# A hybrid decoder block on one core: the recurrent branch's output projection as seven block products per two banks of tokens

## The chip, the cores and the metric

The kernel runs on one core of a Trainium2 chip. TensorE (PE) multiplies, VectorE (DVE), ScalarE (ACT) and GpSimd (POOL) do the elementwise work, and SyncE (SP) issues most DMAs. The metric is the device time of one execution in microseconds (us); lower is better.

## What is computed

One layer of a block with two parallel branches over 2048 tokens of width 1024, all in float32. Cut to what matters here:

```python
h = rms_norm(x, g_norm) * (1 + scale) + shift
x_rnn, z_rnn, q, k, v, z_attn, g_r, g_a = split(h @ w_in)
hr = rg_lru(causal_conv(x_rnn), ...)
y_rnn  = (hr * silu(z_rnn)) @ w_out_rnn        # 2048 x 1024 times 1024 x 1024
o = dilated_attention_mixture(rope(q), rope(k), v)
y_attn = (o * silu(z_attn)) @ w_out_attn
merged = sigmoid(g_r + b_r) * y_rnn + sigmoid(g_a + b_a) * y_attn
out = rms_norm(x + gate * (merged @ w_o), g_final)
```

The change concerns `y_rnn`, the product of the recurrent branch with `w_out_rnn`.

## The kernel before

**Precision.** Each float32 operand is split into a rounded high part and the rest, its low part. A product of two operands is three matmuls (`mm3`, line 154): high by high, high by low, low by high. A split is two operations: the high part by ACT (`hi_act`, 159) or by a DVE reduction over one element (1777), the low part by POOL (`lo_pool`, 165) or DVE (`lo_dve`, 168).

**Stages.** The tokens are two halves of two banks of 512. For each half the input projection runs as pairs of column blocks, each by the seven products of a Strassen-Winograd scheme (`strassen`, 355; products on operands B11, T2, T3, T1, B21, T4, B22). A product is four `mm3`. Small work, such as loads, splits, stores and the recurrence, is hung on product numbers (`after_prod`, `late`, lines 224 to 234; `later`, 1253) and issued when that product has been. At the end of the second half the last 42 products are the rotary pairs of q and k with four plain pairs between them (1363 to 1373). Beside them `residual_gate` (1257) computes the gate vector from eight loads of 512 KB, added by DVE.

**Attention with a fill.** Attention runs in slots, 96 units of scores plus lead-in and lead-out. Between its pieces each slot issues steps of a generator `fill` (`steps`, 1731), which does the output projections: a step is one `mm3` of 512 tokens (line 1840). The rate is `FILL` steps per slot, 2.85 in the first half's heads and 2.75 in the second's (lines 35 and 1888), with a few more at the start. `spend` issues them in three places of a slot: two after the scores, one after the transposes. Everything there is in an order written out by hand, so every engine, and SP's queue, works in program order.

**The fill's jobs.** Four jobs for the recurrent branch (one per bank, from `yaT`), then four for attention (from `oT`), of which the first lies in the slots and the last three follow as a tail of 192 steps, beside which the output projection's weights are built. A job is 64 steps: eight row blocks m of the result, each summed over eight k in one of two `pj` PSUM tiles. Weights come already split from `wD`, 512 KB for half a column of blocks. They are split and stored earlier, beside the second half's input projection (`output_weights`, 428). The operands y of a job are eight tiles of 256 KB; their loads and splits sit at fixed steps around the start of the job (`LOAD_Y`, `SPLIT_Y`, 1871), in nine buffer pairs `yh`, `yl`. `evict` (1792) multiplies a finished tile by its gate, loaded from `grT`, and `store` writes it to `mrT`.

**Winograd's terms.** In the change the same seven products are used for `y_rnn`. B11, B12, B21 and B22 are the blocks of the operand, upper or lower half of the rows by first or second bank of the half; T1 to T4 are their sums and differences.

## Time and profile before

| | |
|---|---|
| median of three runs | 2160.47 us (2158.46 to 2162.48) |
| the profiled execution, its own time | 2161.23 us |
| its span, first to last instruction | 2159.4 us |
| mean granted TensorE clock | 0.998 |
| busy, share of the span | PE 99%, DVE 68%, ACT 60%, POOL 52% |

By stage, from the windows and the timelines: the first half's projection to about 752 us, the second half's to about 1340, attention with the fill from 1340 to 1865, the tail of the fill, then the output projection to the end. PE's busy time counts overlapping matmuls once, so it says that something was under way, not that PE ran at its peak rate. A group's row gives line, engine, operation, output from inputs, shape, count, then busy time and mean time of one, then the idle time of the engine ahead of it and what ended that.

### The profile page before, as it was taken

The page shows a single profiled execution, that of the slowest core. Times are in us where ns is not written, and L with a number is a line of the kernel's source. Part 1 is how long each engine was busy: PE and PEld are TensorE (multiplying, and loading weights), DVE is VectorE, ACT ScalarE, POOL GpSimd, SP SyncE. Part 2 cuts the span into 40 slices and gives each one's busy share as a digit, 9 for nine tenths or more (in the row PEclk, how much of TensorE's full clock was granted, in tenths as well). Part 3 has the DMA queues.
Part 4 walks back from the last instruction along what each step waited for, and adds up shares of the span by engine and source line. Part 5 has one row for each costly group of instructions (what it writes and reads, how often), then busy time and mean ns, then how long its engine had stood idle before and what let it go on. Part 6 is the DMA issues. An engine that isn't in the chain of part 4 may idle for free.

```text
span 2159.4 us, 32571 instructions
## 1 busy us (share of the span) xinstructions
PE 2136.6 (99%) x10539; PEld 1788.3 (83%) x10539; DVE 1463.3 (68%) x2582; ACT 1296.2 (60%) x2592; POOL 1120.6 (52%) x868
## 2 busy tenths in 40 slices
PE   9999999999999999999999999999999999999998
PEld 6888778888888888888888887889898988878887
DVE  6759878768656715544436684587777687788777
ACT  5748668668644527457457532677788888443333
POOL 1467667777666423223223675466666664432555
PEclk9999999999999999999999999999999999999999
DMA  8467887887655368899997676888887777899543
GB/s 301 142 211 256 280 290 264 288 294 244 174 115 166 108 229 291 301 305 311 323 318 240 152 173 171 300 269 263 273 275 218 256 236 239 300 316 300 181 170 114
DMA packets 416575, 521.39 MB, mean 241 GB/s; under 512 B 107574, under 2 KB 282898, under 8 KB 415380
## 3 DMA queue, kind: packets, MB, share of 16 engines
q1 hardware_dynamic: 376388, 401.65, 59.7%
q10 hardware_dynamic: 34384, 99.78, 12.2%
q0 software_dynamic: 5632, 17.88, 2.6%
q8 instruction: 83, 1.36, 0.3%
q14 instruction: 88, 0.72, 0.1%
HBM read 332.02 MB, written 187.17 MB: 240 GB/s over the span
## 4 chain that ended last, share of the span: by engine, by line
PE 71%; DVE 4%; DMA 3%; issue 1%; POOL 1%; ACT 1%; SPq 0%; ACTq 0%; POOLq 0%; DVEq 0%
PE X L152 14%; PE V L152 13%; PE pj L152 12%; PE Z L152 7%; PE W L152 7%; PE Y L152 6%; PE sc L152 4%; PE o L152 4%; PE pg L152 1%; PE pT L1568 1%; PE pT L1581 1%; DMA fg<-gaT 1%; DMA kraw<-kqT 1%; DVE ptl L169 1%; DVE yl L169 1%
## 5 line engine op out<-in xcount | busy, mean ns | idle before, releaser
L166 POOL TENSOR_TENSOR S<-R,S 128x512 fp32r<-128x512 f32 x192 | 295.3, 1546 | 169.3 <-ACT S L160 82.9
L152 PE MATMUL V<-T,S 128*128 128x512 f32 x1344 | 324.3, 390 | 1.9 <-DVE ev L461 1.9
L152 PE MATMUL X<-T,S 128*128 128x512 f32 x1344 | 323.8, 390 | 1.6 <-ACT u L391 1.3
L152 PE MATMUL pj<-yh,S 128*128 128x512 f32 x896 | 321.6, 402 | 1.3 <-DVE fg L1795 0.8
L152 PEld LDWEIGHTS X<-T,S 128*128 128x128 f32 x1344 | 251.8, 188 | 56.5 <-ACT u L391 2.9
L152 PEld LDWEIGHTS V<-T,S 128*128 128x128 f32 x1344 | 251.9, 188 | 55.9 <-issue 1.9
L166 POOL TENSOR_TENSOR S<-s,S 128x512 fp32r<-128x512 f32 x116 | 173.3, 1494 | 150.1 <-ACT S L160 114.3
L152 PEld LDWEIGHTS pj<-yh,S 128*128 128x128 f32 x896 | 168.3, 188 | 32.3 <-DVE S L169 1.3
L1481 ACT ACTIVATE pp<-pp,st 128x256 f32<-128x256 f32 (+3 forms) x256 | 133.8, 524 | 78.0 <-DVE st L1480 77.4
L152 PE MATMUL pj<-yl,S 128*128 128x512 f32 x448 | 175.5, 392 | 1.0 <-POOL yl L166 1.0
L160 ACT ACTIVATE S<-s 128x512 fp32r<-128x512 f32 x124 | 77.3, 624 | 145.1 <-DVE s L291 92.1
L152 PE MATMUL W<-T,S 128*128 128x512 f32 x672 | 161.6, 389 | 0.0
L152 PE MATMUL Y<-T,S 128*128 128x512 f32 x672 | 161.6, 389 | 0.0
L152 PE MATMUL Z<-T,S 128*128 128x512 f32 x672 | 161.4, 389 | 0.0
L160 ACT ACTIVATE S<-R 128x512 fp32r<-128x512 f32 x200 | 121.5, 622 | 59.0 <-DMA R<-in_w_in_dram 14.8
L169 DVE TENSOR_TENSOR ptl<-pT,pth 128x384 fp32r<-128x384 f32 (+1 forms) x160 | 97.8, 628 | 80.5 <-ACT pth L160 78.4
L152 PEld LDWEIGHTS W<-T,S 128*128 128x128 f32 x672 | 126.0, 188 | 26.9 <-issue 0.9
L152 PEld LDWEIGHTS Z<-T,S 128*128 128x128 f32 x672 | 126.2, 188 | 26.2
L152 PEld LDWEIGHTS Y<-T,S 128*128 128x128 f32 x672 | 126.1, 188 | 26.1
L166 POOL TENSOR_TENSOR s<-R,s 128x512 fp32r<-128x512 f32 x32 | 43.2, 1350 | 188.8 <-ACT s L160 164.6
L980 DVE SCALAR_TENSOR_TENSOR xc<-xr,par,xc 128x512 f32<-128x512 f32 x96 | 102.0, 1062 | 52.1 <-ACT xc L974 49.9
L1548 ACT ACTIVATE pp<-pp,M 128x256 f32<-128x256 f32 (+3 forms) x256 | 118.0, 523 | 12.8 <-DVE M L1680 12.8
(419 smaller groups left out, 4906.0 us busy)
## 6 DMA issues: line engine op xcount, KB each, us to landing
sD<-S ACTq DMA_DIRECT2D x140, 512.0 KB, 3.7
S<-sD SPq DMA_DIRECT2D x140, 512.0 KB, 5.0
S<-wD SPq DMA_DIRECT2D x82, 512.0 KB, 5.5
R<-in_w_in_dram SPq DMA_DIRECT2D x144, 256.0 KB, 3.3
wD<-s ACTq DMA_DIRECT2D x64, 256.0 KB, 5.1
kraw<-kqT SPq DMA_DIRECT2D x32, 384.0 KB, 5.1
T<-in_w_mod_dram SPq DMA_DIRECT2D x16, 512.0 KB, 9.1
vN<-ev SPq DMA_DIRECT2D x32, 256.0 KB, 2.7
```

Of the source, the lines that this page charges most:

```text
L152: nc.tensor.matmul(o, lhsT=l, rhs=r, start=st, stop=sp, **kw)
L160: nc.scalar.activation(o, i, AF.Copy)
L166: nc.gpsimd.tensor_tensor(o, i, h.bitcast(F32), ALU.subtract)
L169: return nc.vector.tensor_tensor(o, i, h.bitcast(F32), ALU.subtract).ins
L980: nc.vector.scalar_tensor_tensor(xc, xr[:, i : i + CH], cw(i), xc, ALU.mult, ALU.add)
L1481: nc.scalar.activation(pdst, pdst, AF.Exp, bias=m_, scale=-1.0, accum_out=l_)
L1548: nc.scalar.activation(pp, pp, AF.Copy, scale=w)
L1568: nc.tensor.transpose(pt[:, c0 + j * P : c0 + (j + 1) * P], pp[i][:, k * P : (k + 1) * P], ident)
L1581: nc.tensor.transpose(pt[:, c * P : (c + 1) * P], pp[:, half * P : (half + 1) * P], ident)
```

## The change

The recurrent branch's four jobs become two rounds (one per half of the tokens) of seven block products. A block product is 4 row blocks p by 4 k, that is 16 steps. Its four PSUM tiles are not summed over products in PSUM: each is evicted on its own (`block_evict`), and running sums are kept in SBUF (`U`, `Q`). B11 is copied to U; T2 and T1 are added to U, T3 plus U goes to Q; B21, T1, T4 and B22 complete one of the four results, which is multiplied by its gate and stored.

- The weights are combined into seven blocks per pair of row blocks, split and stored in `wB` by `output_weights`: 28 blocks of 512 KB instead of 16 tiles, with 16 DVE combinations. The attention weights follow at a pitch of 3 products instead of 4.
- The operand sums T1 to T4 are made by `block_sums` beside the last 42 products of the input projection: eight groups, each with four loads, two DVE and two POOL subtracts and four stores of 256 KB to `tB`. The gate's adds are cut to halves of the width and spread over more products.
- An operand takes one of seven buffer pairs (14 tiles; four more hold U). Each block loads the next one's operands behind its steps 1, 4, 7 and 12, and splits at step 1 its own fourth operand, at 6, 9 and 12 the next one's first three. High parts are made by DVE, or by ACT for the even ones of the first round; low parts by POOL.
- `FILL` becomes 2.54 and 2.44.

The core of the diff:

```diff
-FILL = (2.85, 2.75)
+FILL = (2.54, 2.44)
...
+    BLOCKS = (("B11", 0), ("B21", 4), ("T2", 1), ("T3", 2), ("T1", 3), ("T4", 5), ("B22", 6))
+    N_WB = 2 * 7 * KH
...
     def output_weights():
+        n0, PITCH = n_prod[0], 3
...
+        for p in range(KH):
+            v, b = {}, 7 * PITCH * p + (4 * PITCH if p > 1 else 0)
+            load = block_loads([w_out_rnn[0][:, 2 * p * P : 2 * (p + 1) * P]])
+            for d, name, i, half in ((1, "a22", 1, 1), (4, "a21", 1, 0), (6, "a11", 0, 0), (8, "a12", 0, 1)):
+                on_n(b + d, lambda v=v, load=load, name=name, i=i, half=half: v.__setitem__(name, load(i, half)))
...
+            for x, (i, name, *sums) in enumerate((
+                (5, "a22"), (3, "a22", "a21", "a22", ALU.add), (0, "a11"), (1, "a22", "a22", "a11", ALU.subtract),
+                (2, "a21", "a11", "a21", ALU.subtract), (4, "a12"), (6, "a12", "a12", "a22", ALU.subtract))):
+                if sums:
+                    on_n(b + 5 + PITCH * x, lambda combine=combine, name=name, sums=sums: combine(name, *sums))
+                split_and_store(b + 5 + PITCH * x, lambda v=v, name=name: v[name], wB[i, p])
...
+    def block_sums(ep):
+        def load(g, half, j):
+            q, k = divmod(g, KH)
+            n = 2 * q + j
+            raws[g, half, j] = t = T(ep, [P, CH], F32, "bs", bufs=5)
+            nc.sync.dma_start(t[:], yaT[(half * KH + k) * P : (half * KH + k + 1) * P, n * CH : (n + 1) * CH])
+        def combine(g, dst, a, b, eng):
+            eng.tensor_tensor(raws[g, *dst][:], raws[g, *a][:], raws[g, *b][:], ALU.subtract)
+        def store(g, i, src):
+            q, k = divmod(g, KH)
+            nc.scalar.dma_start(tB[q, i, k], raws.pop((g, *src))[:])
+        b11, b12, b21, b22 = (0, 0), (0, 1), (1, 0), (1, 1)
+        dve, pool = nc.vector, nc.gpsimd
+        for g in range(2 * KH):
+            for d, fn, *args in ((-2, load, *b12), (-2, load, *b11), (-2, load, *b22), (-1, load, *b21),
+                                 (0, combine, b11, b12, b11, dve), (0, combine, b12, b22, b12, pool),
+                                 (1, combine, b22, b22, b11, dve), (1, store, 0, b11), (1, store, 2, b12),
+                                 (2, combine, b21, b21, b22, pool), (2, store, 1, b22), (3, store, 3, b21)):
+                later(3 + 5 * g + d, lambda fn=fn, g=g, args=args: fn(g, *args))
...
+        def operand(n, raw=None):
+            g, k = divmod(n, KH)
+            if g < 14:
+                q, (name, _) = g // 7, BLOCKS[g % 7]
+                h, l = OT[n] = fl_pair(n % 7)
...
+        def split(n, raw=None):
+            if n < 14 * KH:
+                h, l = OT[n]
+                src = l[:].bitcast(F32) if raw is None else raw[:]
+                if raw is not None or n % 2 == 0 and n < 7 * KH:
+                    hi_act(h[:], src)
+                else:
+                    nc.vector.tensor_reduce(h[:], src.unsqueeze(2), AX.X, ALU.max)
+                (lo_dve if raw is not None and n > 4 else lo_pool)(l[:], src, h[:])
+        OUT = {"B21": (0, 0), "T1": (1, 1), "T4": (1, 0), "B22": (0, 1)}
...
+        def block_evict(g, p, ps):
+            name = BLOCKS[g % 7][0]
+            tt = nc.vector.tensor_tensor
+            if name == "B11":
+                U[p] = T(fl, [P, CH], F32, f"F{14 + p}")
+                nc.vector.tensor_copy(U[p][:], ps[:])
+            elif name in ("T2", "T1"):
+                tt(U[p][:], ps[:], U[p][:], ALU.add)
+            elif name == "T3":
+                Q[p] = T(pR, [P, CH], F32, f"R{p}")
+                tt(Q[p][:], ps[:], U[p][:], ALU.add)
+            if name in OUT:
+                t = G[g, p]
+                tt(ps[:], ps[:], (Q if OUT[name][0] else U)[p][:], ALU.add)
+                tt(t[:], ps[:], t[:], ALU.mult)
...
+        for g in range(14):
+            for p in range(KH):
+                ps = T(pj, [P, CH], F32, "pj")
+                x = KH * g + p
+                for k in range(KH):
+                    j = KH * p + k
+                    if k == 1:
+                        (load_wb(x + 3) if x + 3 < N_WB else load_w(x + 3 - N_WB))
+                        if last:
+                            block_evict(*last)
...
+                    w, (yh, yl) = W[x], OT[KH * g + k]
+                    mm3(ps[:], w[:, 0, k, :], w[:, 1, k, :], yh[:], yl[:], first=k == 0, last=k == KH - 1)
+                    if k == KH - 1:
+                        W.pop(x)
+                    n = KH * (g + 1)
+                    for at_, k1 in ((1, 0), (4, 1), (7, 2), (12, 3)):
+                        if j == at_ and n + k1 > 6:
+                            operand(n + k1)
+                    for at_, n1 in ((1, n - 1), (6, n), (9, n + 1), (12, n + 2)):
+                        if j == at_ and n1 > 6:
+                            split(n1)
...
+                    yield
+                last = g, p, ps
```

193 lines of the change are left out of this document (125 added, 68 removed).

## The prediction

> **What bounds the kernel now.** I read the page first, its shares and its forty slices, then the chain that ended last, then the windows by stage.
>
> ```profile
> PE 2136.6 (99%) x10539; PEld 1788.3 (83%) x10539; DVE 1463.3 (68%) x2582; ACT 1296.2 (60%) x2592; POOL 1120.6 (52%) x868
> PEclk9999999999999999999999999999999999999999
> L152 PE MATMUL pj<-yh,S 128*128 128x512 f32 x896 | 321.6, 402 | 1.3 <-DVE fg L1795 0.8
> ```
>
> The last row is two thirds of the output projections (the high half of y meets both halves of the weights; the low half is the other third). Its 402 ns is a latency and not a price, since matmuls overlap. The price comes from the chain, where twelve of them follow each other without a gap:
>
> ```profile
> 788.07 2.72 PE W L152 x12
> ```
>
> 2.72/12 = 0.2267 us for each 512-column matmul, so one step (three matmuls, line 1840) costs 0.68 us. Whether steps can be saved at that price depends on whether TensorE is full in the stage they lie in.
>
> ```profile
> 780.00:1130.00 350.00, 350.00 (x1543) 289.44 (x1542) 164.74 (x224) 198.62 (x307) 99.21 (x76) 1.00 0.92 307
> 1226.00:1300.00 74.00, 74.00 (x328) 61.29 (x327) 54.77 (x66) 23.56 (x43) 49.76 (x33) 1.00 0.75 177
> 1300.00:1340.00 40.00, 40.00 (x172) 31.20 (x171) 20.68 (x27) 11.04 (x20) 23.24 (x16) 1.00 0.59 167
> 1340.00:1865.00 525.00, 519.34 (x3359) 464.51 (x3358) 380.21 (x1099) 399.72 (x1113) 311.39 (x270) 1.00 0.82 259
> 1422.00:1494.00 72.00, 72.00 (x491) 65.23 (x490) 50.92 (x176) 57.12 (x186) 44.99 (x47) 1.00 0.84 267
> 1404.00:1422.00 18.00, 17.16 (x114) 14.89 (x113) 17.38 (x48) 13.27 (x41) 11.61 (x11) 1.00 0.89 264
> 1512.00:1530.00 18.00, 17.33 (x115) 14.83 (x114) 16.24 (x49) 12.46 (x40) 9.36 (x9) 1.00 0.92 283
> 1620.00:1638.00 18.00, 15.55 (x99) 13.69 (x97) 14.00 (x41) 12.11 (x33) 13.18 (x13) 0.93 0.67 198
> ```
>
> Columns: length; busy time and instructions of PE, weight loads, DVE, ACT, POOL; clock; DMA share; GB/s. The first three stretches are the input projection of the second half. The fourth is attention with 320 output-projection steps filled in. In the quiet fifth, attention runs at 491/72 = 6.8 matmuls per us without idle time; so TensorE binds there, and a step removed is 0.68 us gained. The last three are the joints between jobs of 64 steps, where eight operands are split within some twenty steps: DVE reaches 17.38 of 18 us and TensorE gets 114, 115 and 99 matmuls where 123 would fit.
>
> **The matmuls.** Before, the recurrent branch takes 4 banks x 8 x 8 = 256 steps. After, 2 x 7 products x 16 = 224. 32 steps x 0.68 = 21.8 us less. The Trainium skill ("TensorE: Matmul & The Clock Gate", Back-to-back issue gap) gives about 131 ns for a 512-column matmul in a sustained stream; by it the saving would be 12.6 us (an estimate). The trace has 226.7 ns here, so its number stands.
>
> **The fill rate.** Slots now take 2.54 and 2.44 steps instead of 2.85 and 2.75. Summed over slots that gives the 288 steps needed, so nothing is left over or moves to the tail. The quiet slot shrinks from 72 us/(46 steps/2.85) = 4.46 to about 4.25 us by the shares (138 of its 491 matmuls write pj).
>
> ```profile
> 1422.00:1494.00 72.00, 38.71 (x138) 23.59 (x138) 4.11 (x6) 1.00 0.84 267
> L1795 DVE TENSOR_TENSOR fg<-pj,fg 128x512 f32<-128x512 f32 x40 | 27.3, 683 | 0.5 <-PE pj L152 0.5
> L1777 DVE TENSOR_REDUCE yh<-R 128x512 fp32r<-128x512 f32 x32 | 21.5, 677 | 0.0
> L166 POOL TENSOR_TENSOR yl<-R,yh 128x512 fp32r<-128x512 f32 x21 | 27.6, 1314 | 19.1 <-DMA vraw<-vN 5.6 <-DVE yh L1777 4.4 <-PE sc L152 3.2
> L169 DVE TENSOR_TENSOR yl<-R,yh 128x512 fp32r<-128x512 f32 x18 | 17.3, 967 | 0.6
> ```
>
> **Evictions.** Each output tile was one multiply of 683 ns, 32 in all. Now every product tile has its own: one operation for B11, T2 and T3, three for T1, two for B21, T4 and B22, that is 12 per pair of rows and 96 in all. 64 x 0.683 = 43.7 us more on DVE.
>
> **Splits.** 56 operands instead of 32. DVE reduces go from 24 to 39 (+10.2 us), DVE low parts from 15 to 2 (-12.6 us at 967 ns), POOL low parts from 17 to 54 (+48.6 us at 1314 ns), ACT high parts from 8 to 17 (ACT is busy 400 of 525). So DVE gains some 41 us and POOL 49 in a stage where they are busy 380 and 311 of 525: none reaches the stage's length on average. By block it is closer. A block of 16 steps lasts 6.3 slots, 26.8 us. DVE has (50.92 - 4.11)/16.1 = 2.9 us a slot of attention, 18.3 a block; a T1 block adds 12 x 0.683 + 4 x 0.677, to 29.2 us, so it is full; B21, T4 and B22 come to 26.5 and B11, T2, T3 to 23.7. I charge 1 us for the two T1 blocks, because DVE catches up while TensorE stands in the waits below; bounds 0 and 5 (the excess of 2.4 us, twice).
>
> **The new wait.** This decides. The fourth operand of each block lies in the buffer of the first operand of the block before, so its load is issued behind step 12, its split only behind step 1 (DVE reduce, then POOL), and step 3 multiplies it: one whole step lies between, where the old table leaves two. TensorE runs in order, so transposes, sums and scores queue behind a late low part. How long does such a split take from the end of the step that issued it?
>
> ```profile
> 1393.53 0.40 PE L152 MATMUL pj<-yh,S 128*128 128x512 f32 x1
> 1393.13 0.68 DVE L1777 TENSOR_REDUCE yh<-R 128x512 fp32r<-128x512 f32 x1
> 1396.72 1.31 POOL L166 TENSOR_TENSOR yl<-R,yh 128x512 fp32r<-128x512 f32 x1
> 1414.87 0.39 PE L152 MATMUL pj<-yh,S 128*128 128x512 f32 x1
> 1415.33 0.62 PE L152 MATMUL pj<-yh,S 128*128 128x512 f32 x2
> 1416.03 0.40 PE L152 MATMUL pj<-yh,S 128*128 128x512 f32 x1
> 1416.84 0.39 PE L152 MATMUL pj<-yl,S 128*128 128x512 f32 x1
> 1417.06 0.39 PE L152 MATMUL pj<-yh,S 128*128 128x512 f32 x1
> 1418.94 0.68 DVE L1777 TENSOR_REDUCE yh<-R 128x512 fp32r<-128x512 f32 x1
> 1419.38 0.40 PE L152 MATMUL pj<-yh,S 128*128 128x512 f32 x1
> 1419.76 1.29 POOL L166 TENSOR_TENSOR yl<-R,yh 128x512 fp32r<-128x512 f32 x1 [1.85 <-PE sc L152]
> 1419.85 0.62 PE L152 MATMUL pj<-yh,S 128*128 128x512 f32 x2
> 1421.10 0.50 PE L152 MATMUL pj<-yl,S 128*128 128x512 f32 x1 [0.62 <-POOL yl L166]
> 1731.53 0.39 PE L152 MATMUL pj<-yh,S 128*128 128x512 f32 x1
> 1733.77 0.68 DVE L1777 TENSOR_REDUCE yh<-R 128x512 fp32r<-128x512 f32 x1
> 1734.53 1.30 POOL L166 TENSOR_TENSOR yl<-R,yh 128x512 fp32r<-128x512 f32 x1 [2.58 <-DVE yh L1777]
> ```
>
> The timelines of TensorE, DVE and POOL hold 16 POOL splits behind a reduce, four of which stand alone; these are the first and the last of the four, and between them one from a joint. Step end to low part done: 1398.03 - 1393.76 = 4.3, 1421.05 - 1416.26 = 4.8, 1735.83 - 1731.76 = 4.1 us. The four alone, as the new ones mostly stand, average 3.6, all sixteen 4.6. The middle one shows the mechanism at work: it had two steps between, and TensorE still waited 0.62 us. What lead is there with one step? A slot issues its steps in three places: two in a row after the scores (A, B), one after the transposes (C), then sums and scores follow. From these rows: a split behind A is needed in C, 1416.84 - 1415.56 = 1.3 us later; behind B in the next A, 1419.61 - 1416.26 = 3.4; behind C in the next B, 1420.31 - 1417.29 = 3.0. The pacing code with the new rates puts the thirteen blocks' step 1 at A followed by B and C three times (2.9 us short each), behind B three times (0.8 twice, 0 in the longer slots of the second half), behind C before A and B twice (1.2 each), behind C with a skipped place or in the longer slots three times (0.3 each), and twice into the first slots, where steps run back to back but DVE is almost idle (reduce plus low part, 2.0, and some queueing, less 0.9 lead: 1.5 each). I take 4.2 us for the split: 3.6, and most of the eviction that is issued just ahead of it (0.68 to 2.05 us), less what DVE does before the step ends. Sum: 8.7 + 1.6 + 2.4 + 0.9 + 3.0 = 16.6 us. Bounds: 0, if DVE and POOL run ahead, and 42 us, with the 4.6 of the crowded splits plus the mean eviction of 1.2 (4.5 x 3 + 2.4 x 3 + 2.8 x 5 + 3.5 x 2).
>
> **The joints go.** The three old joints inside the recurrent branch cost (123 - 114), (123 - 115) and some 20 matmuls of 0.147 us, 5.4 us together, some of it the start of the longer heads and a clock of 0.93. I credit two thirds, 3.6 us (0 to 5.4).
>
> **Weights, earlier.** 28 blocks are split and stored instead of 16 tiles, with 16 combinations on DVE. That lies in 780 to 1130, where DVE is busy 47% and POOL 28% under a TensorE without idle time: nothing. Its 6.3 MB more are 6.3/(307/0.92) = 19 us of DMA in a stretch with 8% x 350 = 28 free. If that cover went, the operand loads would be late by the excess.
>
> **Block sums, in the last pairs of the projection.** 32 loads and 32 stores of 256 KB, 16 subtracts on DVE and 16 on POOL, eight rounds of five products (13.6 us each).
>
> ```profile
> L299 DVE TENSOR_TENSOR R<-R,R 128x512 f32<-128x512 f32 x5 | 7.4, 1488 | 0.0
> gw<-in_w_mod_dram SPq DMA_DIRECT2D x8, 512.0 KB, 4.6
> ```
>
> At 1.49 us, the nearest row, DVE goes from 54.77/74 = 74% to about 74 + 2 x 1.49/13.6 = 96%, less the gate's adds being spread further. The Trainium skill ("SBUF — State Buffer", Who interferes with whom) says why such a subtract can take 1.5 instead of 0.68 us: a DVE operation with two SBUF inputs and a POOL operation that reads SBUF block each other; the trace agrees (L299 is 0.65 to 1.78 us over the run, the evictions from PSUM stay at 0.68). DMA: 16.8 MB at 334 GB/s are 50 us in 114, on top of shares of 0.75 and 0.59; 0.75 x 13.6 + 2.1 MB/0.334 is 16.5 us in a round of 13.6; the gate's loads move later, so some 2.5 us too much in each of the first five rounds. What hides it: operands are loaded four products (10.9 us) ahead and land in some 5, and each PSUM tile has several products until its next use. Bounds 0 and 12.5 us; I take 2.5, near zero, because TensorE has no idle time at all there now. SP carries the loads, ACT's queue the stores; a store that waits for POOL holds ACT, which is busy only 32%.
>
> **Sum.** -21.8 + 16.6 + 1 - 3.6 + 2.5 = -5.3 us on the profiled execution of 2161.23 (span 2159.4, 1.8 outside), which is 0.8 above the median of the runs. From the median: 2160.5 - 5.3 = 2155.2.
>
> **Rivals.**
>
> *The late operand eats the saving.* If the split takes 5 us or more behind its step, thirteen waits cost 28 to 42 us. For it: DVE and POOL both get fuller, and the eviction stands ahead of the reduce. Against: the splits are spread evenly, no longer eight at a joint. The fourth operand's load has five steps to land in, 8 us, but SP is one queue and any wait on it eats into that. The point from which the kernel is slower: (21.8 + 3.6 - 1 - 2.5)/13 = 1.7 us per block; mine is 1.3. At 2.7 us per block, 35 us: 2155.2 + 18.5 = 2174.
>
> *The wait is covered.* If DVE and POOL run ahead, the waits stay under 5 us: 2160.5 - 21.8 - 3.6 + 5 + 1 = 2141.1, the projection free. For it: in two of the four lonely splits the reduce began before its step had ended. Against: the low part still needs 2 us, more than the lead of an A.
>
> *The projection becomes DMA-bound.* The 2.5 us of excess in five rounds come through, 12.5 us: 2155.2 + 10 = 2165.2. For it the share of 0.75; against it the prefetch.
>
> *The change does not remove the steps.* Only if the pacing left steps over for the tail; counted out, it doesn't (2160 then).
>
> **Chances.** My sum or near it, 0.42; the late operand 0.24; the covered wait 0.20; the projection 0.12; none 0.02. A measurement of this kernel tells about 0.2%, 4.3 us, from no change. My own case straddles that: 0.26 of its 0.42 below -4.3 us, 0.14 within, 0.02 above. So faster 0.26 + 0.20 = 0.46; within 0.14 + 0.03 (late operand) + 0.05 (projection) + 0.02 = 0.24; slower 0.30. My case alone spans 2148 to 2162; the range for eight in ten takes in most of both sides, 2140 to 2175.
>
> **What would show it.** The pj matmuls fall by 96. DVE's busy time in the stage rises by about 41 us, POOL's by 49. TensorE waits for POOL's low part about once per block, at its fourth step, 1 to 3 us, and longest where the block's step 1 falls on A; if those waits total over 25 us, the first rival is right; under 5, the second. The stretch from 780 to the start of attention keeps its length within 3 us; if it grows by 8 or more, the third. I'd be wrong altogether if TensorE waited in the stage on something else: on evictions (two pj buffers, now turned over every four steps), or DVE on an operand's load behind SP's waits.

## The result, and the profile after

The changed kernel takes 2235.17 us (median of four, 2229.59 to 2239.78) against 2160.32 us (four runs of the kernel before on the same chip): a ratio of 1.0345, 95% interval 1.0319 to 1.0371. The forecast was 2155.2, with a range of 2140 to 2175. The profiled execution took 2234.06 us, its span is 2232.2.

First the page of the profile: the three lines that answer to those shown of the kernel before.

```profile
PE 2153.1 (96%) x10443; PEld 1786.2 (80%) x10443; DVE 1552.3 (70%) x2688; ACT 1306.5 (59%) x2613; POOL 1205.4 (54%) x933
...
PEclk9999999999999999999999989999999999999999
...
L154 PE MATMUL pj<-F,S 128*128 128x512 f32 x1248 | 337.3, 405 | 24.8 <-POOL F L168 13.5
```

TensorE has 96 matmuls less, as it should, and yet more busy time, partly because it ran at a lower clock for a while (the 8 in the clock's row). It also stands 24.8 us ahead of the output projections' matmuls, where it stood 2.3 (1.3 in the row shown of the kernel before and 1.0 in that of the low half).

To place the loss I cut the span at two marks that both kernels have: the last matmul into V (the projection's last product) and the last softmax (DVE's custom operation). A line's own view gives a row's first and last start. Before:

```profile
L152 PE MATMUL V<-T,S x1344: 387/389/481, 133.0 to 1340.2; 128*128 128x512 f32 x192
```

```profile
L1480 DVE CUSTOM_DVE_ANT_0 pp<-sc,msk x256: 273/420/692, 1357.2 to 1826.1; 128x256 f32<-128x256 f32 x56, 128x128 f32<-128x128 f32 x40, 128x384 f32<-128x384 f32 x32
```

After:

```profile
L154 PE MATMUL V<-T,S x1344: 387/389/794, 133.1 to 1382.9; 128*128 128x512 f32 x192
```

```profile
L1546 DVE CUSTOM_DVE_ANT_0 pp<-sc,msk x256: 275/419/692, 1403.1 to 1899.3; 128x256 f32<-128x256 f32 x56, 128x128 f32<-128x128 f32 x40, 128x384 f32<-128x384 f32 x32
```

| stage | before | after | difference | forecast |
|---|---|---|---|---|
| to the projection's last matmul | 1340.2 | 1382.9 | +42.7 | +2.5 |
| from there to the last softmax ("attention" below) | 485.9 | 516.4 | +30.5 | -7.8 |
| from there to the end of the span | 333.3 | 332.9 | -0.4 | 0 |

Now the windows of the first two stages, with the columns of the prediction's windows. Before:

```profile
1226.00:1340.60 114.60, 114.60 (x501) 93.01 (x500) 75.45 (x91) 34.62 (x63) 73.60 (x49) 1.00 0.69 174
1340.60:1826.50 485.90, 480.31 (x3104) 429.75 (x3104) 355.96 (x1052) 375.14 (x1060) 293.12 (x256) 1.00 0.81 259
```

After:

```profile
1226.00:1383.30 157.30, 134.04 (x516) 103.40 (x514) 102.89 (x117) 33.73 (x60) 95.84 (x64) 0.90 0.79 226
1383.30:1899.70 516.40, 479.83 (x3007) 419.30 (x3008) 397.17 (x1118) 383.53 (x1077) 340.41 (x296) 0.98 0.78 253
```

In the projection's tail TensorE is idle for 157.3 - 134.0 = 23.3 us, and its clock averages 0.90, worth about 0.10 x 157 = 16 us more. Yet no engine is full there (DVE 65%, POOL 61%) and DMA works at 0.79. That is the mark of queues that wait for each other. The waits of that stretch (engine, line, for what: us in total, times, longest):

```profile
DVE bs L1341 <- DMA bs<-yaT: 23.3, 5, 7.3
ACT S L162 <- DMA tB<-bs: 23.1, 3, 12.2
...
POOL bs L1341 <- DVE bs L1341: 12.5, 5, 6.7
...
PE V L154 <- DVE t L496: 10.6, 5, 4.6
...
PE pg L154 <- DVE gacc L1310: 5.8, 2, 3.0
```

Read from the top it looks like a chain: DVE waits for a block's rows, POOL for DVE's subtract, ACT behind a store of the results, and TensorE for an eviction (`t`, line 496) that DVE has behind the subtract. One round in the timeline (start, length, engine, line, what, idle time before):

```profile
1291.31 1.66 SPq L1338 DMA_DIRECT2D bs<-yaT  x3
...
1296.53 0.69 DVE L1341 TENSOR_TENSOR bs<-bs,bs 128x512 f32<-128x512 f32 x1 [3.96 <-DMA bs<-yaT]
1297.13 0.68 DVE L301 TENSOR_TENSOR R<-R,R 128x512 f32<-128x512 f32 x1
...
1297.30 1.64 POOL L1341 TENSOR_TENSOR bs<-bs,bs 128x512 f32<-128x512 f32 x1 [6.66 <-DVE bs L1341]
1297.74 0.68 DVE L496 TENSOR_TENSOR t<-V,u 128x512 f32<-128x512 f32 x1
...
1298.34 1.15 DVE L1310 SCALAR_TENSOR_TENSOR gacc<-gw,ca,gacc 128x512 f32<-128x512 f32 x1
...
1299.54 1.02 PE L154 MATMUL pg<-gacc,ones 128*1 128x512 f32 x2 [2.99 <-DVE gacc L1310]
1299.55 0.63 ACT L162 ACTIVATE S<-R 128x512 fp32r<-128x512 f32 x1 [6.84 <-DMA tB<-bs]
...
1300.49 3.91 PE L154 MATMUL X<-T,S 128*128 128x512 f32 x9
```

DVE stood 3.96 us for the rows, with an operand sum, an eviction and a gate addition behind it, and all of them came late. TensorE then stood 2.99 us for the gate's addition, although the gate and the block sums share nothing but DVE's queue and the transfers. Not every wait of TensorE stands right behind late rows: its longest here, 4.61 us for `t` before 1286.55, came when DVE had worked without a pause since 1278.3, four of its five operations before `t` taking 1.74 to 1.81 us each.

In attention the count of matmuls fell as forecast (96 fewer into pj in the whole run, 94 of them among those recorded between the marks), and the loads of the engines rose as forecast: DVE by 397.2 - 356.0 = 41.2 us (forecast 41), POOL by 47.3 (forecast 49). The waits of TensorE's matmuls there and the groups of the new work:

```profile
PE pj L154 <- POOL F L168: 13.5, 16, 2.2
PE pj L154 <- DVE F L1896: 9.6, 7, 3.1
```

```profile
L1896 DVE TENSOR_REDUCE F<-F 128x512 fp32r<-128x512 f32 x39 | 26.4, 677 | 0.0
...
L1928 DVE TENSOR_TENSOR fg<-pj,fg 128x512 f32<-128x512 f32 x32 | 22.1, 691 | 1.1
...
L168 POOL TENSOR_TENSOR F<-F,F 128x512 fp32r<-128x512 f32 x49 | 63.1, 1289 | 66.6 <-DVE F L1896 37.3 <-ACT F L162 16.8 <-DMA vraw<-vN 4.0
```

POOL's 49 low parts are the operands 7 to 55 in order; laid beside TensorE's waits, twelve of the thirteen blocks have a wait at their fourth operand, 0.2 to 2.1 us for POOL and up to 3.1 for DVE ahead of it, 19.4 of the 23.1 us in all. One of them in the timeline:

```profile
1541.35 0.69 DVE L1927 TENSOR_TENSOR pj<-pj,R 128x512 f32<-128x512 f32 x1
...
1542.07 0.69 DVE L1928 TENSOR_TENSOR fg<-pj,fg 128x512 f32<-128x512 f32 x1
1542.68 0.68 DVE L1896 TENSOR_REDUCE F<-F 128x512 fp32r<-128x512 f32 x1
...
1543.41 0.50 PE L154 MATMUL pj<-F,S 128*128 128x512 f32 x1 [1.52 <-DVE F L1896]
1543.43 1.27 POOL L168 TENSOR_TENSOR F<-F,F 128x512 fp32r<-128x512 f32 x1 [1.77 <-DVE F L1896]
...
1544.76 0.73 PE L154 MATMUL pj<-F,S 128*128 128x512 f32 x2 [0.86 <-POOL F L168]
```

Two evictions, then the reduce, then POOL; TensorE stands for each in turn.

### The profile page after: what moved, and what is told of

Same layout as the page of the kernel before. It is cut to its first block, busy times and chain, and to the rows that moved or that the text cites. A ratio compares the mean times of both kernels' runs of the same rounds, so it can differ in the third digit from the quotient of the medians.

```text
span 2232.2 us, 32850 instructions
## 1 busy us (share of the span) xinstructions
PE 2153.1 (96%) x10443; PEld 1786.2 (80%) x10443; DVE 1552.3 (70%) x2688; ACT 1306.5 (59%) x2613; POOL 1205.4 (54%) x933
## 5 line engine op out<-in xcount | busy, mean ns | idle before, releaser
L154 PE MATMUL pj<-F,S 128*128 128x512 f32 x1248 | 337.3, 405 | 24.8 <-POOL F L168 13.5
L154 PE MATMUL V<-T,S 128*128 128x512 f32 x1344 | 332.8, 397 | 17.7 <-DVE t L496 10.6
L154 PE MATMUL X<-T,S 128*128 128x512 f32 x1344 | 328.4, 393 | 5.4 <-ACT S L162 2.7
L154 PEld LDWEIGHTS V<-T,S 128*128 128x128 f32 x1344 | 257.1, 192 | 76.2 <-issue 16.3
L154 PEld LDWEIGHTS pj<-F,S 128*128 128x128 f32 x1248 | 225.0, 191 | 74.7 <-POOL F L168 20.0
L168 POOL TENSOR_TENSOR s<-R,s 128x512 fp32r<-128x512 f32 x44 | 61.4, 1396 | 205.9 <-ACT s L162 90.0
L1546 DVE CUSTOM_DVE_ANT_0 pp<-sc,msk 128x256 f32<-128x256 f32 (+3 forms) x256 | 103.5, 447 | 20.6 <-PE sc L154 19.4
```

The source lines that it names most:

```text
L154: nc.tensor.matmul(o, lhsT=l, rhs=r, start=st, stop=sp, **kw)
L168: nc.gpsimd.tensor_tensor(o, i, h.bitcast(F32), ALU.subtract)
L1546: nc.vector.tensor_tensor_reduce(pdst, s_ps, mask, 1.0, 3e38, ALU.add, ALU.min, m_)
```

## The experiments

The kernels fall into two groups, one for each stage. This table has the median and the three stages of all of them; marks and stages are those of the table above, taken from each kernel's profile, so from one execution each. How far a mark can be trusted shows in the ten kernels whose attention is that of the kernel after (after, e1, e2, e4, e7, e8, e11 to e14): their attention column goes from 514.2 to 527.3.

| run | edit in a few words | median | last V | attention | rest |
|---|---|---|---|---|---|
| before | | 2160.3 | 1340.2 | 485.9 | 333.3 |
| after | | 2235.2 | 1382.9 | 516.4 | 332.9 |
| e1 | no block sums | 2196.1 | 1342.1 | 519.2 | 332.6 |
| e2 | no gate | 2222.1 | 1361.1 | 527.3 | 332.9 |
| e4 | stores on POOL's queue | 2239.0 | 1385.3 | 521.8 | 334.2 |
| e7 | no gate, loads two products earlier | 2210.3 | 1352.4 | 518.9 | 332.9 |
| e8 | half tiles, loads one product earlier | 2245.1 | 1383.3 | 523.0 | 332.9 |
| e11 | gate loads one product later | 2229.7 | 1378.4 | 523.2 | 333.5 |
| e12 | no subtracts | 2219.7 | 1361.5 | 524.9 | 332.9 |
| e13 | no subtracts, no gate | 2206.2 | 1341.9 | 524.1 | 334.5 |
| e14 | half of the block sums | 2212.1 | 1372.4 | 514.2 | 333.7 |
| e3 | fourth operand early | 2228.1 | 1379.4 | 505.6 | 343.4 |
| e5 | no block sums, operand early | 2187.3 | 1344.0 | 501.6 | 340.1 |
| e6 | e5, one eviction per output | 2165.3 | 1343.6 | 482.1 | 341.9 |
| e9 | e6, no low parts on POOL | 2158.1 | 1341.9 | 473.2 | 340.4 |
| e10 | no block sums, eviction behind the reduce | 2188.6 | 1342.3 | 508.6 | 334.1 |
| e16 | no block sums, one eviction, operand late | 2171.0 | 1341.5 | 494.3 | 333.0 |
| e15 | both repairs, nothing left out | 2222.3 | 1373.1 | 506.1 | 341.1 |

### The projection's tail

**e1: without the block sums.**

```diff
-            block_sums(qp)
...
-                    src = (tB[q, int(name[1]) - 1, k] if name[0] == "T" else
-                           yaT[(i * KH + k) * P : (i * KH + k + 1) * P, ...])
+                    i, j = i % 2, j % 2
+                    src = yaT[(i * KH + k) * P : (i * KH + k + 1) * P, ...]
```

> The block sums are left out (no loads, subtracts and stores in the projection's last pairs); the T products read rows of the gated recurrence as they are, so their sums are not those of the reference. In the profile after, the projection's last matmul starts 43 us later than before and attention lasts 30 us longer. Theory A (the block sums and their waits cost the projection's 43 us): about 2192 us, the projection ends near 1340, attention still 30 us too long. Rival B (the gate of the residual, now loaded with two products' pitch in halves, costs the 43): above 2220. If attention also shortens by more than 5 us, its loss had come partly from the projection.

Measured: 2196.09 us (2195.43 to 2197.08), ratio 1.0165 (1.015 to 1.018).

```profile
L154 PE MATMUL V<-T,S x1344: 387/389/504, 133.1 to 1342.1; 128*128 128x512 f32 x192
```

```profile
L1545 DVE CUSTOM_DVE_ANT_0 pp<-sc,msk x256: 274/419/693, 1359.8 to 1861.3; 128x256 f32<-128x256 f32 x56, 128x128 f32<-128x128 f32 x40, 128x384 f32<-128x384 f32 x32
```

Theory A holds. The projection ends 40.8 us earlier, 1.9 us from where it ended before, so the gate's new pitch and the 28 weight blocks that are made earlier cost next to nothing by themselves. Attention keeps its loss (519.2 where it was 516.4): the two losses are separate, and each can be studied without the other.

**e2: without the gate.**

```diff
-            w["acc"] = T(ep, [P, CH], F32, "gacc")
...
-            nc.vector.tensor_tensor(w["row"][:], w["pt"][:1, :], w["row"][:], ALU.add)
...
-            for k in range(KT):
-                y = q * KT + k
-                later(1 + 2 * y, lambda q=q, k=k: load(q, k))
-                later(5 + 2 * y, lambda q=q, k=k: add(q, k))
-            later(20 + 16 * q, total)
```

> The residual's gate keeps only its bias row: its 16 weight loads, 16 accumulations on DVE and two column sums are left out; the block sums stay. Theory A1 (block sums are loaded one or two products ahead and land later than that, so DVE, POOL and ACT wait in order; the gate is a bystander): 5 to 10 us less than after, about 2227. Rival A2 (SP holds its queue for the gate's next load until DVE has added, and the operand and block loads wait behind it, so that the ring closes only with the gate): 25 to 43 us less, 2192 to 2210.

Measured: 2222.08 us, 13 less than after; the projection ends at 1361.1, 21.8 earlier, of which attention gives 10.9 back.

```profile
L154 PE MATMUL V<-T,S x1344: 387/389/629, 132.9 to 1361.1; 128*128 128x512 f32 x192
```

Neither number was right in time, but in the stage that it concerns leaving out the gate takes away half of the loss, although e1 shows that it costs nothing when the block sums are gone. So it is no bystander, and A1 as I had put it is too narrow.

**e11: is it SP's wait that ties the gate in?** In the kernel after, SP waits for the gate's additions before it can issue the next load:

```profile
SPq L1303 <- DVE gacc L1310: 15.9, 4, 5.1
```

```diff
-                later(1 + 2 * y, lambda q=q, k=k: load(q, k))
+                later(2 + 2 * y, lambda q=q, k=k: load(q, k))
```

> The kernel after, with each load of the gate's weights one product later, so that SP no longer issues it right behind the addition that frees its buffer. Nothing is left out. Theory A2 (SP stands in its queue until DVE has added, and the block and operand loads stand behind it; without the gate the projection ended 22 us earlier): 8 to 20 us less than after, 2215 to 2227, SP's waits for that addition from 19 us to under 6. Rival (the gate's cost is DVE's additions themselves, 16 of some 1.1 us and their waits for loads that now come later): within 5 us of after, or slower.

Measured: 2229.74 us (2223.61 to 2236.97), ratio 1.0318 (1.0287 to 1.0349), which overlaps that of after; the projection ends 4.5 us earlier. SP's waits for the gate are gone: the longest of them is now another line's.

```profile
SPq L1191 <- DVE t L1186: 8.9, 4, 3.4
```

So 19 us of SP's waiting (15.9, and 3.0 for the first addition) were worth some 5 us, if any. A2 forecast 2215 to 2227 and falls as the account of the gate's 22 us.

**e4: do the stores hold ACT?**

```diff
-            nc.scalar.dma_start(tB[q, i, k], raws.pop((g, *src))[:])
+            nc.gpsimd.dma_start(tB[q, i, k], raws.pop((g, *src))[:])
```

> The 32 stores of block sums are issued from POOL's queue instead of ACT's; nothing is left out. Rival A3 (a store that waits for a subtract holds ACT, and with it the high parts of the projection's operands and the evictions): 10 to 25 us less than after, 2210 to 2225. Theory A1 (late loads hold DVE and POOL first, ACT only inherits it): within 8 us of after, perhaps slower, because now POOL's splits stand behind the stores that wait for DVE.

Measured: 2239.00 us (2237.01 to 2243.04), 4 more than after, with ranges that overlap. ACT no longer stands behind the stores, but it stands 48.6 us for DVE's line 293 instead, where it was 11.7. So the 23.1 us were inherited from what DVE does late, and A3 falls.

**e12 and e13: the transfers without those who wait for them.** In e12 the subtracts go, and in e13 the gate's loads and additions as well (the edit of e2).

```diff
-            eng.tensor_tensor(raws[g, *dst][:], raws[g, *a][:], raws[g, *b][:], ALU.subtract)
+            pass
```

> The kernel after, with the 32 subtracts of the block sums left out; its loads and stores stay, so rows are stored as they were read and T products are not those of the reference. Theory A1 (DVE and POOL stand in order before subtracts whose rows are late): 25 to 40 us less than after, 2196 to 2210, the projection ends before 1358. Rival A4 (16.8 MB more in the DMA queues, and SP's and ACT's waits for them): 2222 or more, the projection ends after 1370.

> The block sums' loads and stores alone: their subtracts are left out, and the gate keeps only its bias row (so T products and the gate are not the reference's). With both left in, the projection's last matmul stands at 1382.9, without the gate at 1361.1, without the subtracts at 1361.5, without all of the block sums at 1342.1. Theory A1 (transfers cost only through instructions of DVE and POOL that stand in order before them; two streams of such instructions, subtracts and gate additions): 1342 to 1347, about 2198. Rival A4 (the transfers cost some 19 us by themselves, through the operand loads and the stores behind them): 1355 or later, 2210 or more.

Measured: 2219.70 and 2206.17 us. The marks of e12 and of e13:

```profile
L154 PE MATMUL V<-T,S x1344: 387/389/504, 132.9 to 1361.5; 128*128 128x512 f32 x192
```

```profile
L154 PE MATMUL V<-T,S x1344: 387/389/497, 133.3 to 1341.9; 128*128 128x512 f32 x192
```

```profile
L1539 DVE CUSTOM_DVE_ANT_0 pp<-sc,msk x256: 276/420/693, 1369.4 to 1866.0; 128x256 f32<-128x256 f32 x56, 128x128 f32<-128x128 f32 x40, 128x384 f32<-128x384 f32 x32
```

With all 16.8 MB still moving, but no instruction of DVE or POOL waiting for them and no gate, the projection ends at 1341.9, where it ends without block sums. Set side by side, the runs give the time of the last V:

| | with the gate | without |
|---|---|---|
| loads, subtracts, stores | 1382.9 | 1361.1 |
| loads and stores | 1361.5 | 1341.9 |
| none | 1342.1 | |

Without the gate, the transfers of the block sums cost this mark nothing. The subtracts cost 19.2 us, the gate another 19.6, and they add up to 41. For the subtracts the instructions alone were taken out; the gate's additions went together with its 16 loads, and no run separates the two. In e12, where the gate is the only one left, it is DVE's gate additions that stand:

```profile
DVE gacc L1310 <- DMA gw<-in_w_mod_dram: 14.8, 5, 6.8
```

So the likely account is that the transfers make rows late (the gate's land in 4.1 us at the median in e12 and in 2.9 in e1), and that a late row costs where an engine that also evicts for TensorE stands in order before it. By time neither side was right: e12 (2219.7) and e13 (2206.2) both lie between the forecasts of A1 and A4. The transfers do cost something behind the mark: in e13 the first softmax follows the last V by 1369.4 - 1341.9 = 27.5 us instead of the 17.7 of e1, and until 1370 ACT waits 12.6 us for DMAs ahead of the first operands' splits, against 1.0 in e1. Of these 10 us some 5 are left at the last softmax (524.1 against 519.2). The medians of e13 and e1 are 10.1 us apart, the profiled executions 6.5.

**e7: more lead.** The gate's room pays for three more buffers.

```diff
-            raws[g, half, j] = t = T(ep, [P, CH], F32, "bs", bufs=5)
+            raws[g, half, j] = t = T(ep, [P, CH], F32, "bs", bufs=8)
...
-            for d, fn, *args in ((-2, load, *b12), (-2, load, *b11), (-2, load, *b22), (-1, load, *b21),
+            for d, fn, *args in ((-4, load, *b12), (-4, load, *b11), (-4, load, *b22), (-3, load, *b21),
```

> Gate left out as in the second experiment (2222.1, projection's last matmul at 1361); in the room that it leaves, eight instead of five buffers for the block sums, and every load two products (5.4 us) earlier; subtracts and stores where they were. Theory A1 (late loads make the waits): the projection ends near 1342, waits of DVE and POOL for these loads under 10 us in sum, time 2196 to 2205. Rival A4 (the transfers themselves are too many: DMA is full): the loads land as late as before, 2215 or more.

Measured: 2210.31 us, between the two. Two products of lead (5.4 us) take back 8.7 of the 19.2 us that the subtracts cost without the gate. Lead helps, and isn't all: DVE and POOL still wait 13.2 and 8.6 us for rows (21.1 and 12.5 in e2), and the subtracts' own time on both engines and their handing over stay. No run separates these.

**e8: more lead in the room that there is.** Tiles of 256 columns, ten of them, loads at -3 and -2 products, sixteen rounds at a pitch of 2.4.

```diff
-            raws[g, half, j] = t = T(ep, [P, CH], F32, "bs", bufs=5)
+            raws[g, half, j] = t = T(ep, [P, CW], F32, "bs", bufs=10)
...
-                later(3 + 5 * g + d, lambda fn=fn, g=g, args=args: fn(g, *args))
+                later(4 + 12 * g // 5 + d, lambda fn=fn, g=g, args=args: fn(g, *args))
```

> Nothing left out: the block sums in half tiles of 256 columns, ten buffers in the same room, loads one product more ahead of the subtracts, sixteen rounds of 2.4 products. Gate as in the kernel after. Theory A1 (lead): 15 to 30 us below after, 2205 to 2220, though the gate's part stays. Rival A4 (DMA) or the doubled count of instructions and transfers: 2235 or more.

Measured: 2245.13 us, 10 more than after: a miss for A1. POOL's waits for DVE's subtracts rise from 12.5 to 36.3 us, and a subtract of half the width is no cheaper on DVE at the median:

```profile
L1343 DVE TENSOR_TENSOR bs<-bs,bs x32: 403/888/1523, 1237.8 to 1385.1; 128x256 f32<-128x256 f32 x32
```

In the kernel after the full width has 678/693/1779 ns (minimum, median, maximum). On POOL the median falls from 1658 to 982 ns. The likely reason, not shown, is that small tiles lose in twice as many handings over what they give in lead.

**e14: half of the sums at half the density.**

```diff
-        for g in range(2 * KH):
+        for g in range(KH):
...
-                later(3 + 5 * g + d, lambda fn=fn, g=g, args=args: fn(g, *args))
+                later(3 + 10 * g + d, lambda fn=fn, g=g, args=args: fn(g, *args))
```

> Half of the block sums, those of the first two banks, at half the density: four rounds of ten products instead of eight of five, the gate as in the kernel after. The sums of the other two banks are left out (their T products use the first ones). Theory F (the loss comes from rounds that follow so closely that each starts late from the one before): the projection ends by 1352, 2205 or less. Rival (each round costs its 5 us by its own waits, whatever the pitch): it ends near 1362, about 2215.

Measured: 2212.14 us (2208.31 to 2222.14; the profiled execution is the longest of them, which may be why its projection ends as late as 1372.4). By the medians four rounds cost (2212.1 - 2196.1)/4 = 4.0 us each and eight cost (2235.2 - 2196.1)/8 = 4.9. So the price is mostly a round's own, and spreading the rounds saves little. The rival comes nearer by the time (about 2215); its mark, 1362, isn't met in the one execution that was profiled.

### Attention

**e3 and e5: the fourth operand early.** An eighth low buffer, F18, beside the seven high ones (`op_pair`) lets a block's fourth operand be loaded behind step 9 and split behind step 14 of the block before. The room comes from the gates' ring, and each gate of the recurrent branch is loaded one tile later. e5 is the same without block sums, and has F18 back as a fourth gate buffer once the recurrent branch is done.

```diff
-                h, l = OT[n] = fl_pair(n % 7)
+                h, l = OT[n] = op_pair(n)
...
-                    for at_, k1 in ((1, 0), (4, 1), (7, 2), (12, 3)):
+                    for at_, k1 in ((1, 0), (4, 1), (7, 2), (9, 3)):
...
-                    for at_, n1 in ((1, n - 1), (6, n), (9, n + 1), (12, n + 2)):
+                    for at_, n1 in ((6, n), (9, n + 1), (11, n + 2), (14, n + 3)):
```

> Only attention: an eighth low buffer (and three gate buffers instead of four) lets the fourth operand of a block be loaded behind step 9 and split behind step 14 of the block before, two steps ahead of the old place, with three steps between split and use. Nothing is left out. Theory C (the fourth operand's split costs nearly all of the loss, by the wait and by the clock that falls after it: 23 us of waits plus 9 us of clock and their tails): 30 to 45 us less than after, about 2197, TensorE's waits on F from 23 us to under 6. Rival D (DVE and POOL are too full with evictions and splits, wherever the split stands): under 10 us less, 2225 or more, the waits move to other operands and to softmax.

> Block sums left out as in the first experiment (so T products read rows as they are), and the fourth operand early as in the third, but with the gates of the attention branch in a ring of four buffers again. The third experiment took 11 us from attention (505.6 from the projection's last matmul to the last softmax, against 516.7) and lost 11 behind it, where a gate load in a ring of three waited for a store and held SP's queue ahead of the weights. Theory (that wait was all of the loss behind attention): 2185, 11 below the run without sums (2196.1), 332 us behind the last softmax. Rival (the early operand's buffers delay the next branch's operands whatever the gates do): 2196, 343 behind it.

Measured: 2228.09 and 2187.31 us. Attention is 10.8 us shorter in e3, and 17.6 in e5 (501.6 against e1's 519.2):

```profile
L1545 DVE CUSTOM_DVE_ANT_0 pp<-sc,msk x256: 275/420/693, 1361.8 to 1845.6; 128x256 f32<-128x256 f32 x56, 128x128 f32<-128x128 f32 x40, 128x384 f32<-128x384 f32 x32
```

TensorE's waits on F fall from 22.5 us in e1 to 6.4 (5.1 for operands, 1.3 for an eviction into an F tile). Theory C gave the operand nearly all of the loss, and falls: about half of it stays. e3's time is the one that D forecast, and as D said a part of the waits moved: TensorE's waits for POOL's q go from 2.0 to 6.0 us. Behind attention both lose some 8 to 11 us in the stage called rest, where e5's theory had forecast nothing (340 against its 332), so a ring of three gate buffers isn't the whole cause of that. I have not settled what is; in e5 TensorE stands 3.3 us there for one split of weights that were loaded late, and 332 us became 340.

**e6, e16 and e9: the evictions and the low parts.** e6 is e5 with the sums left out of the evictions. e16 has that edit with the operand in its late place, and so with the gates' ring as in the kernel after. e9 is e6 without POOL's low parts.

```diff
-            if name == "B11":
-                U[p] = T(fl, [P, CH], F32, f"F{14 + p}")
-                nc.vector.tensor_copy(U[p][:], ps[:])
-            elif name in ("T2", "T1"):
-                tt(U[p][:], ps[:], U[p][:], ALU.add)
-            elif name == "T3":
...
-                tt(Q[p][:], ps[:], U[p][:], ALU.add)
             if name in OUT:
                 t = G[g, p]
-                tt(ps[:], ps[:], (Q if OUT[name][0] else U)[p][:], ALU.add)
                 tt(t[:], ps[:], t[:], ALU.mult)
```

> As the run beside it (no block sums, fourth operand early), and the products' sums are left out too: an output product is multiplied by its gate and nothing else, so DVE has 32 evictions of 0.68 us in the branch instead of 96, as before the change; the output lacks the sums. Theory D (the 64 extra evictions fill DVE, and splits, softmax and sums wait behind them): 15 to 25 us below that run, attention 480 to 490. Rival D2 (the splits on POOL and the operand order carry what is left): within 5 us of that run.

> Block sums and the products' sums left out (32 evictions, one multiply each), the fourth operand in its old, late place. With the sums in and the operand late attention took 519.2 us, with the operand early 501.6, with both edits 482.1. Theory G (two causes that add up: the operand's place costs 17 us whatever DVE has to do): 499 to 503 us of attention. Rival H (one cause: the operand is late only because evictions stand ahead of its reduce on DVE): below 488. Rival H2 (the evictions cost only as they make the operand late; so without the early place they cost more): between.

> As the run with one eviction (no block sums, fourth operand early, output products only multiplied), and the 49 low parts of 1.29 us that POOL makes of the recurrent branch's operands are left out: the low tile keeps the loaded rows, so the products are not those of the reference. That run still has 482 us from the projection's last matmul to the last softmax where 465 would be left if TensorE never waited. Theory E (POOL, 44 us busier than before, makes its splits and the casts of q late): 465 to 472, about 2155 in all. Rival E2 (ACT's and DVE's share, or the bursts in which steps now come): within 4 us of that run (2165.3).

Measured: 2165.33, 2170.96 and 2158.12 us. The softmax rows of e6 and of e16:

```profile
L1545 DVE CUSTOM_DVE_ANT_0 pp<-sc,msk x256: 279/420/693, 1363.5 to 1825.7; 128x256 f32<-128x256 f32 x56, 128x128 f32<-128x128 f32 x40, 128x384 f32<-128x384 f32 x32
```

```profile
L1545 DVE CUSTOM_DVE_ANT_0 pp<-sc,msk x256: 279/420/693, 1359.8 to 1835.8; 128x256 f32<-128x256 f32 x56, 128x128 f32<-128x128 f32 x40, 128x384 f32<-128x384 f32 x32
```

The row of e9:

```profile
L1545 DVE CUSTOM_DVE_ANT_0 pp<-sc,msk x256: 280/420/694, 1360.7 to 1815.1; 128x256 f32<-128x256 f32 x56, 128x128 f32<-128x128 f32 x40, 128x384 f32<-128x384 f32 x32
```

The 64 extra evictions (43.7 us of DVE) cost 19.5 us of attention with the operand early, as theory D forecast, and 24.9 with it late. The operand's place costs 17.6 us with all evictions and 12.2 without the extra ones. Of 37.1 us together some 5 may be common to both, which is no more than these marks scatter. H, one cause for all, falls. e16's 494.3 misses G's number (499 to 503) and lies in the stretch left to H2, but H2's mechanism, that the evictions cost only as they make the operand late, doesn't fit: they cost 19.5 with the operand early too. So there are two causes, with a share in common that isn't settled. Without POOL's low parts another 8.9 us go, near to what theory E forecast (473.2 where it gave 465 to 472); by the medians it is 7.2. Even then 473.2 remain, where 485.9 less 94 x 0.2267 would be 464.6.

**e10: the eviction behind the reduce.**

```diff
                     if k == 1:
...
-                        if last:
-                            block_evict(*last)
+                    if k == 2 and last:
+                        block_evict(*last)
```

> Block sums left out; the fourth operand in its old place, but the eviction of the product before is issued behind that operand's reduce instead of ahead of it (behind step 2 instead of 1). Beside the run without sums (2196.1). Theory C2 (part of the operand's lateness is the one to three evictions that stand ahead of its reduce on DVE, 1.2 us on average): 8 to 15 us less, 2181 to 2188. Rival C3 (the lead of one step is too short whatever stands ahead; the waits are for the step that frees the buffer and for POOL): within 4 us, 2192 to 2200.

Measured: 2188.59 us, 7.5 below e1, with attention 10.6 us shorter and waits for the evictions in their place (TensorE's weight loads stand 15.1 us for `fg`, line 1927 there). It is nearly what C2 forecast, for a move by one step that takes no buffer.

**e15: both repairs in the kernel after** (the edits of e5's operand and of e11).

> Nothing left out: the fourth operand early (with four gate buffers behind the branch) and the gate's loads a product later, in the kernel after. By the single runs -9 and -5 us, about 2220. If it falls below 2160 the change can be repaired by places alone; theory: it can't, because 64 evictions (19 us), the low parts (9 us) and most of the block sums (some 35 us) remain against the 21 us saved: 2215 to 2225. Should the two repairs hinder each other behind attention: 2230.

Measured: 2222.32 us, ratio 1.0289 (1.0274 to 1.0305). As expected it stays far above 2160 and within 2215 to 2225. No version here that leaves nothing out beats the kernel before.

## Why the prediction was wrong

Point by point, in the order of its sum:

- **Matmuls, -21.8.** The count is right: 96 matmuls fewer, 94 of them recorded between the marks, 21.3 us. The price of 226.7 ns is the trace's own; no run isolates it, and the sum of attention below leaves 6 us open.
- **The new wait, +16.6.** Right in place and cause, and in size as a sum: at the fourth operand of twelve of the thirteen blocks, 19.4 us of visible waits (0 to 3.9 a block, where the sum had 0 to 2.9), and 12.2 to 17.6 us of attention when it is taken away (e16 against e6, e1 against e5).
- **DVE full, +1, bounds 0 and 5.** This step failed. I compared DVE's work with the length of a block, found only the T1 blocks full, and charged their excess. The runs show 19.5 to 24.9 us for the 64 evictions, at a DVE that is busy 77% of the stage. An eviction costs when it stands ahead of something that TensorE needs soon (e10 shows one such place), well before DVE is full. What failed is the assumption that an engine's work costs only as much as it exceeds the block's length.
- **POOL's 49 us more, at nothing.** The same failure in small: 8.9 us (e9), with TensorE's waits for POOL's q gone from 3.5 us to none.
- **The old joints, -3.6.** No run isolates it. What is left of attention's sum is -21.3 + 17.6 + 19.5 + 8.9 = 24.7 against 30.5 measured; the other 6 us aren't accounted for. (The three prices were measured from e1, whose attention is 2.8 us longer than that of the kernel after, so from there it is 9.)
- **Weights earlier, 0.** Right: without the block sums the projection ends within 1.9 us of its old place.
- **Block sums, +2.5, bounds 0 and 12.5.** This is the step that failed most: 40.8 us. I had priced it as bytes over a rate and as DVE's share of a round, and the third rival with it. The work was not under-rated: DVE's subtracts took 1.16 us in the mean, less than the 1.49 that I had. The transfers alone cost nothing up to the last V (e13). What I wrote hides it, operands loaded four products ahead and PSUM tiles with several products to spare, does hide late operands; it doesn't help DVE, which evicts TensorE's tiles in the same queue in which it waits for a block's rows. In the program the rows are asked for two products (5.4 us) ahead of their first subtract (three for B21; the forecasts above call this one or two), and they landed in 5.3 us at the median (the last column of the DMA issues of that stretch):

```profile
bs<-yaT SPq DMA_DIRECT2D x32, 256.0 KB, 5.3
```

  So there was no slack, and the lead of the program was not that of the engines: in six of the eight rounds DVE stood ready for the first subtract between 2.4 us before and 3.7 us after SP issued the first of its loads (1.3 us after it in the round shown). I had the lead and the landing time of the operands in the text and never put those of the block sums beside each other. Why SP comes so late is open, since taking away its waits for the gate gave 4.5 us (e11); and how much of the subtracts' 19.2 us is late rows and how much their own work is shown only as far as e7 goes, 8.7.
- **A store that waits for POOL holds ACT.** I named it and let it go, rightly as far as e4 shows.

The signs given beforehand read well. The pj matmuls, DVE's and POOL's busy times came out within 2 us; the waits on F, 23.1 us, stayed just under the 25 that would have meant the first rival; the stretch to the start of attention grew by 43 us, far over the 8 that were to mean the third rival, in its place but not by its mechanism.

## What to carry to other kernels

For each instruction that is added to an engine's queue, ask when its input lands and what stands behind it; an engine at 65% that waits in order for a row that is 4 us late makes its consumers late just as a full one does. A stream that is harmless alone, as the gate was in e1, can cost its waits once another is added beside it: take out the streams and the transfers separately, as in the table above, before blaming bandwidth. And the longest waits of a profile (SP's 19 us, ACT's 23) may be inherited: taking them away, or moving them to another queue, changed the time by about 5 us, no more than the executions of one kernel differ.

## What the runs showed of the hardware

A wait of TensorE can cost more than its length, since the granted clock fell after some of them. The windows of the kernel after around one wait (length, busy time and matmuls of PE, clock, DMA share, GB/s):

```profile
1738.00:1742.30 4.30, 4.30 (x28) 1.00 0.60 161
1742.30:1744.20 1.90, 0.02 (x1) 1.00 1.00 343
1744.20:1745.00 0.80, 0.67 (x1) 0.62 0.98 361
1745.00:1751.00 6.00, 5.42 (x23) 0.50 0.98 303
1752.00:1756.00 4.00, 4.00 (x31) 1.00 0.87 320
```

And around another of nearly the same length, where it did not fall:

```profile
1814.50:1816.50 2.00, 0.09 (x2) 1.00 0.71 194
1816.50:1824.00 7.50, 7.50 (x57) 1.00 0.87 244
```

In the first case a pause of 1.9 us was followed by some six us at half clock, worth 3 us more; in the second the clock stayed at 1.00. It fell after six waits of attention's stage. What decides it, these runs don't show. The Trainium skill ("TensorE: Matmul & The Clock Gate", What's actually happening) has the gate fall to half after an idle window of about 3.4 us and return after a busy one; the two levels agree with the trace, but in the first case the fall came after a pause shorter than that window and lasted longer, with short pauses within it. Over the two stages the lower clock is worth some 16 and 10 us, an estimate from the mean clocks (0.10 x 157 and 0.02 x 516).
